# Memory-attention scores by seven products of halves: one more stage of a hybrid decoder step brought to the seven-product scheme

## The chip, the cores and the metric

The kernel runs on one core of a Trainium2 chip, in one launch. Its engines work side by side, each through its own queue of instructions: TensorE (PE in the profile; its weight loads are listed as PEld), VectorE (DVE), ScalarE (ACT), GpSimd (POOL) and SyncE (SP), which here issues the DMA transfers. The metric is device time in microseconds, lower is better.

## What is computed

One layer of a decoder for a prompt of 2048 tokens of width 1024, and for 8 x 4 new tokens of other requests. A mixer (gated linear attention beside a spatial-gating MLP) and its output projection are followed by a cross attention over 256 memory tokens, and by a gated feed-forward part with a short convolution. The change is about the cross attention of the prompt:

```python
def mem_attend(hn, mk, mv, wq_x, wo_x):
    B, T, _ = hn.shape
    q = (hn @ wq_x).reshape(B, T, MEM_HEADS, MEM_DH)
    s = jnp.einsum('bthd,bmhd->bhtm', q, mk).astype(jnp.float32) * (MEM_DH ** -0.5)
    p = jax.nn.softmax(s, axis=-1).astype(mv.dtype)
    o = jnp.einsum('bhtm,bmhd->bthd', p, mv).reshape(B, T, D_MODEL)
    return o @ wo_x
```

Here `hn` is the normed residual, there are 4 heads of 256, and `mk`, `mv` are projections of the 256 memory tokens. All values are float32.

## The kernel before

**Precision.** Each float32 matrix product is made of three matmuls on operands split into a high and a low part (`mm3`, lines 92 to 94: high by high, high by low, low by high). A split (`split`, lines 84 and 85) is a copy on ScalarE for the high part and a subtraction on VectorE for the low one.

**Tiling.** The prompt is worked in four sub-blocks of 512 tokens. In a sub-block: input projection, mixer, output projection (`w1`, `w2`: tiles `a_wo`), scores (`sc`), softmax, turning of the probabilities (`pT`), attention output (`x1`, `x2`: tiles `a_wx`), feed-forward (`a_wg`, `a_wup`, `d`). The 32 other tokens ride with the second and third sub-block.

**Folded keys.** In the first sub-block the query weights are multiplied with the keys once (`turn_wq`, `fold_qk`), head by head, so that the scores of two heads are the product of the tokens (512 x 1024) and a matrix of 1024 x 512, two heads of 256 memory tokens. The folded keys are split, written to DRAM (`qkd`) and read back in every sub-block, high and low part (`wready`). The values are folded with the output weights in the same way (`vod`).

**Scores.** Step `score(i, j)` takes two heads (i) and a quarter of the 1024 rows (j). For each of four chunks of 128 tokens it accumulates into one PSUM bank: tokens are the stationary operand, 512 key columns the moving one. At the last quarter `soften` takes maxima from PSUM, exponentiates into a scratch tile and divides by the sum. `turn` transposes the probabilities on TensorE.

**Tokens.** `out_proj_steps` adds the projection to the residual, column block m by column block, and calls `finish(m)`: scaling by the norm's gain, the split, the square, and the sum of the squares on GpSimd. The row scale of the norm is applied later, in the softmax.

**Seven products.** The feed-forward stage of sub-blocks 1 to 3 multiplies 2 x 2 blocks by seven products instead of eight (`seven_step`), with sums and differences of blocks on both sides. `seven_tokens` makes those of the tokens from an even and an odd column block (the halves of the contraction) and two halves of the tokens, as the split operands named A11, S1, A12, S2, S3, S4, A22. The sums of the weights were made once and lie in DRAM.

**Order and buffers.** `run` walks through a list of steps and issues the loads of the steps ahead (`AHEAD = 5` units); `weave` mixes side steps into the main list. The compiler's scheduler then orders each engine's instructions along a simulated timeline, so neighbours in the program may change places. Buffers that matter: 5 each of high weights, low weights and raw weights, 49 tiles of 128 x 544 (`U`), 6 scratch tiles of that size (`T_`), 4 key reload tiles (`X`), 4 PSUM banks for accumulators (`acc`) and 4 for the rest (`mps`).

Of the kernel before, what the change touches and what calls it, by code (L numbers as in the profile page):

```python
# [37 lines left out]
def hymba_step_kernel(  # L38
# [142 lines left out]
    def seven_tokens(a, b, H, name):  # L181

        B11, B12, B21, B22 = a[:, :H], a[:, H:2 * H], b[:, :H], b[:, H:2 * H]
        t13, t24 = T_(f"t13{name}"), T_(f"t24{name}")
        lo_, hi_ = slice(0, H), slice(H, 2 * H)
        dve.tensor_tensor(t13[:, lo_], B12, B11, ALU.subtract)
        dve.tensor_tensor(t13[:, hi_], B22, B12, ALU.subtract)
        dve.tensor_tensor(t24[:, lo_], B22, t13[:, lo_], ALU.subtract)
        dve.tensor_tensor(t24[:, hi_], B21, t24[:, lo_], ALU.subtract)
        one = U(f"w1{name}", F32R)  # L190
        split(one[:, lo_], one[:, hi_], B11)
        out = {"A11": (one[:, lo_], one[:, hi_])}
        for nm, src, first, second in (("b", b, "A12", "S4"), ("t", t13, "S1", "S3"), ("u", t24, "S2", "A22")):
            h, l = U(f"w{nm}h{name}", F32R), U(f"w{nm}l{name}", F32R)
            split(h[:, :2 * H], l[:, :2 * H], src[:, :2 * H])
            out[first], out[second] = (h[:, lo_], l[:, lo_]), (h[:, hi_], l[:, hi_])
        return out
# [296 lines left out]
    qkd = [[dp.tile([128, 2, 2, 512], F32, tag=f"qkd{i}{j}", name=f"qkd{i}{j}") for j in range(4)] for i in range(2)]  # L494
# [86 lines left out]
    def turn_wq(h, j, raw):  # L581

        out = []
        if j == 0:
            again("k", h)
# [9 lines left out]
    def fold_qk(h, j):  # L595

        kh, kl = mem_st.t["k"]
        w = mem_st.t.pop(("w", h, j))
        flush()
        for kk in range(2):  # L600
            ps = mps(f"qkp{h}{j}{kk}")
# [6 lines left out]
            hi, lo = U(f"qkh{h}{j}{kk}", F32R), U(f"qkl{h}{j}{kk}", F32R)  # L608
            split(hi[:, :512], lo[:, :512], ps)
            for x, t in enumerate((hi, lo)):  # L610
                put(qkd[h // 2][2 * j + kk][:, x, :, (h % 2) * 256:(h % 2 + 1) * 256],
                    t[:, :512].bitcast(F32).rearrange("p (k m) -> p k m", k=2))
# [27 lines left out]
    for h in range(4):  # L640
        for j in range(2):
            qk_steps.append(Step(lambda a, h=h, j=j: turn_wq(h, j, a), [wraw_unit(wq_x[0], 4 * j, 4, h * 256, 256, f"wqf{h}{j}")]))
            qk_steps.append(Step(lambda h=h, j=j: fold_qk(h, j)))
# [535 lines left out]
    def out_proj_steps(B, unit, src, g, name, sample, first, finished, keep=None, seven=False,  # L1179
# [35 lines left out]
        def finish(m):  # L1215
            if seven:
                t = T_(f"{name}g{s}{m}")
                act.activation(t[:, :T], B.h[m][:, :T], AF.Copy, scale=gcol(g, m))
                if m % 2:
                    B.hn.append(seven_tokens(B.even, t, T // 2, f"{s}{m}"))  # L1220
                else:
                    B.even = t
# [35 lines left out]
    def attention_steps(B):  # L1258
# [15 lines left out]
        def score(i, j):  # L1274

            def fn(wu):
                wh, wl = wu
                for c in range(4):
                    cs = slice(c * 128, (c + 1) * 128)
                    if j == 0:  # L1280
                        B.p[i, c] = acc(f"sc{s}{i}{c}")
                    ps = B.p[i, c]
                    for kk in range(2):
                        k = 2 * j + kk
                        mm3(ps, B.hn[k][0][:, cs], B.hn[k][1][:, cs], wh[:, kk], wl[:, kk], k == 0, k == 7)
                    if j == 3:
                        soften(i, c, ps)
            return Step(fn, [wready(qkd[i][j], f"qk{s}{i}{j}")])

        def soften(i, c, ps):  # L1290

            mx = narrow(f"mx{s}{i}{c}")
            dve.tensor_reduce(mx[:, 0:2], ps.rearrange("p (t m) -> p t m", t=2), AX.X, ALU.max)
            dve.tensor_scalar(mx[:, 0:2], mx[:, 0:2], B.rn[:, c:c + 1], None, ALU.mult)
            p = T_(f"p{s}{i}{c}")
            for hh in range(2):
                hs_ = slice(hh * 256, (hh + 1) * 256)
                act.activation(p[:, hs_], ps[:, hs_], AF.Exp,
                               bias=mx[:, hh:hh + 1], scale=B.rp[:, c:c + 1], accum_out=mx[:, 2 + hh:3 + hh])
            dve.reciprocal(mx[:, 4:6], mx[:, 2:4])  # L1300
            for hh in range(2):
                pt = p[:, hh * 256:(hh + 1) * 256]
                dve.tensor_scalar(pt, pt, mx[:, 4 + hh:5 + hh], None, ALU.mult)
            B.p[i, c] = p

        def turn(h):
            for mt in range(2):
                ps = mps(f"pT{s}{h}{mt}")
                for c in range(4):
                    a = (h % 2) * 256 + mt * 128  # L1310
                    pe.transpose(ps[:, c * 128:(c + 1) * 128], B.p[h // 2, c][:, a:a + 128], ident)
# [4 lines left out]
        return Step(scales), [score(i, j) for i in range(2) for j in range(4)], [Step(lambda h=h: turn(h)) for h in range(4)]  # L1316
# [341 lines left out]
    for s, B in enumerate(blocks):  # L1658
# [5 lines left out]
        if B.mix_sample:  # L1664
            def keep():
                if not hasattr(smp, "x"):
# [3 lines left out]
                                      lambda B=B: B.cat, "gx", "wo", B.mix_sample, 4, B.mix_sample, keep)  # L1670
# [6 lines left out]
        steps += weave(sc + x1, (turns[:2], 4, 5), (turns[2:], 8, 8))  # L1677
# [49 lines left out]
```

## Time and profile before

| | |
|---|---|
| median of 3 runs | 2845.88 us (2843.69 to 2846.43) |
| the profiled execution | 2846.04 us, of which the span is 2844.3 |
| mean granted clock of TensorE | 0.997 |
| score stages (first to last score matmul) | 324.8 to 371.9, 1028.4 to 1076.1, 1722.3 to 1769.3, 2393.7 to 2440.5 us |
| DMA | 625.54 MB, 219 GB/s over the span |

A row of a group names the line, engine, operation, what is written and read, the shape and the count; then the busy time in us and the mean duration of one in ns; then how long the engine had been idle before, and what ended that. Durations of matmuls overlap: what one costs is the distance to the next.

### The profile page before, as it was taken

What the parts mean: (1) busy time and instruction counts of PE and PEld (TensorE: products, weight loads), DVE (VectorE), ACT (ScalarE), POOL (GpSimd) and SP (SyncE); (2) the same over time, 40 slices, a digit from 0 to 9 for tenths busy, and PEclk for the clock granted to TensorE, in tenths of its full rate; (3) what the DMA queues carried; (4) which work ended last, traced back from release to release, by engine and by line L of the source; (5) the groups of instructions that cost most, each with busy time, mean ns of one, the idle gap of its engine ahead of it and who ended that gap; (6) DMA issues with size and microseconds to landing.
All of it is one profiled execution on the core that took longest, in us unless ns stands there. A gap on an engine that the chain in (4) does not pass through costs nothing.

```text
span 2844.3 us, 45766 instructions
## 1 busy us (share of the span) xinstructions
PE 2814.4 (99%) x17366; PEld 2457.6 (86%) x17366; DVE 1773.6 (62%) x3160; ACT 1047.0 (37%) x1942; POOL 542.4 (19%) x617
## 2 busy tenths in 40 slices
PE   8999999999999999999999999999999999999998
PEld 8788888888888898898888888899999888899998
DVE  6577468777657735555555773666666674565555
ACT  5536334333363424222124443422223543331221
POOL 1002113111110211322220021322221012131221
PEclk9999999999999999999999999999999999999999
DMA  9656679999932245888994215577776323577784
GB/s 304 207 156 199 208 228 332 335 340 329 345 112 77 94 153 178 302 284 291 329 344 161 73 60 181 191 259 257 257 263 213 104 69 119 185 258 269 273 286 173
DMA packets 363920, 625.54 MB, mean 220 GB/s; under 512 B 26730, under 2 KB 235724, under 8 KB 363702
## 3 DMA queue, kind: packets, MB, share of 16 engines
q1 hardware_dynamic: 363702, 622.62, 64.6%
q8 instruction: 138, 2.26, 0.3%
q14 instruction: 80, 0.66, 0.1%
HBM read 497.21 MB, written 125.31 MB: 219 GB/s over the span
## 4 chain that ended last, share of the span: by engine, by line
PE 95%; DVE 2%; DMA 1%; ACT 1%; issue 1%; POOL 0%; SPq 0%; DVEq 0%; POOLq 0%; ACTq 0%
PE d L92 6%; PE d L94 6%; PE d L93 6%; PE a_wo L92 2%; PE a_wo L94 2%; PE a_wo L93 2%; PE sc L94 2%; PE sc L93 2%; PE sc L92 2%; PE a_wx L93 2%; PE a_wx L94 2%; PE a_wx L92 2%; PE s L1022 2%; PE a_wg L92 1%; PE a_wup L92 1%; PE a_wg L93 1%
## 5 line engine op out<-in xcount | busy, mean ns | idle before, releaser
L92 PE MATMUL d<-acth,whi_wd 128*128 128x512 f32 (+2 forms) x720 | 244.6, 340 | 0.5 <-DVE h L1581 0.5
L93 PE MATMUL d<-actl,whi_wd 128*128 128x512 f32 (+2 forms) x720 | 242.5, 337 | 0.0
L94 PE MATMUL d<-acth,wlo_wd 128*128 128x512 f32 (+2 forms) x720 | 242.0, 337 | 0.0
L1581 DVE TENSOR_TENSOR h<-d,h 128x512 f32<-128x512 f32 (+1 forms) x232 | 133.4, 582 | 139.6 <-PE d L94 139.4
L1520 POOL TENSOR_TENSOR c<-c,bc_f 128x512 f32<-128x512 f32 (+1 forms) x88 | 138.5, 1578 | 137.9 <-ACT c L1519 137.2
L94 PEld LDWEIGHTS d<-acth,wlo_wd 128*128 128x128 f32 x720 | 135.4, 188 | 15.3 <-issue 1.2
L92 PEld LDWEIGHTS d<-acth,whi_wd 128*128 128x128 f32 x720 | 135.3, 188 | 14.4 <-DVE h L1581 0.7
L93 PEld LDWEIGHTS d<-actl,whi_wd 128*128 128x128 f32 x720 | 135.6, 188 | 13.8 <-issue 0.4
L1510 ACT ACTIVATE c<-g,colsb 128x512 f32<-128x512 f32 x88 | 71.7, 815 | 203.7 <-DVE g L1479 151.8
L1542 POOL TENSOR_TENSOR c<-r_q_wup,c 128x512 f32<-128x512 f32 (+1 forms) x33 | 59.1, 1790 | 333.5 <-DVE r_q_wup L279 213.1
L92 PE MATMUL a_wo<-ch,h_wo 128*128 128x512 f32 (+1 forms) x320 | 112.7, 356 | 4.5 <-DVE r L828 4.5
L1507 POOL COPY carry<-g 128x2 f32<-128x2 f32 x88 | 30.7, 349 | 436.5 <-DVE g L1479 434.4
L94 PE MATMUL a_wo<-ch,l_wo 128*128 128x512 f32 (+1 forms) x320 | 112.4, 353 | 0.0
L93 PE MATMUL a_wo<-cl,h_wo 128*128 128x512 f32 (+1 forms) x320 | 112.0, 351 | 0.0
L1511 DVE SCALAR_TENSOR_TENSOR c<-g,colsb,c 128x512 f32<-128x512 f32 x88 | 86.0, 977 | 29.3 <-ACT c L1510 28.8
L92 PE MATMUL sc<-whi_qk,woh 128*128 128x512 f32 x256 | 102.1, 399 | 0.0
L92 PE MATMUL a_wx<-pTh,whi_wx 128*128 128x512 f32 x256 | 101.3, 396 | 0.0
L94 PE MATMUL sc<-whi_qk,wol 128*128 128x512 f32 x256 | 101.1, 397 | 0.0
L93 PE MATMUL a_wx<-pTl,whi_wx 128*128 128x512 f32 x256 | 101.1, 395 | 0.0
L93 PE MATMUL sc<-wlo_qk,woh 128*128 128x512 f32 x256 | 101.0, 395 | 0.0
L94 PE MATMUL a_wx<-pTh,wlo_wx 128*128 128x512 f32 x256 | 100.6, 393 | 0.0
L84 ACT ACTIVATE acth<-c 128x512 fp32r<-128x512 f32 (+1 forms) x88 | 55.9, 636 | 110.4 <-DVE c L1542 85.0
(3369 smaller groups left out, 9204.8 us busy)
## 6 DMA issues: line engine op xcount, KB each, us to landing
whi_wd<-wd SPq DMA_DIRECT2D x66, 512.0 KB
wlo_wd<-wd SPq DMA_DIRECT2D x66, 512.0 KB
r_wo<-in_w_out_dram SPq DMA_DIRECT2D x32, 512.0 KB
whi_qk<-qkd SPq DMA_DIRECT2D x32, 512.0 KB
wlo_qk<-qkd SPq DMA_DIRECT2D x32, 512.0 KB
wlo_wx<-vod SPq DMA_DIRECT2D x32, 512.0 KB
whi_wx<-vod SPq DMA_DIRECT2D x32, 512.0 KB
r_wg<-in_w_gate_dram SPq DMA_DIRECT2D x22, 512.0 KB
```

The source lines that it names most:

```text
L84: act.activation(hi, src, AF.Copy)
L92: pe.matmul(ps, wh, xh, start=first, stop=False)
L93: pe.matmul(ps, wh, xl, start=False, stop=False)
L94: pe.matmul(ps, wl, xh, start=False, stop=last)
L1022: pe.matmul(ps3[:, :, c * 64:(c + 1) * 64], kl[:, c * 128:(c + 1) * 128], kr3[:, :, c * 64:(c + 1) * 64], start=True, stop=True)
L1507: pool.tensor_copy(carry[:, f, :], g[:, SB:SB + 2])
L1510: act.activation(c[:, :SB], g[:, 2:SB + 2], AF.Identity, bias=cb, scale=w2)
L1511: dve.scalar_tensor_tensor(c[:, :SB], g[:, 1:SB + 1], w1, c[:, :SB], ALU.mult, ALU.add)
L1520: pool.tensor_tensor(c[:, :T], c[:, :T], B.fbc[:, :T], ALU.mult)
L1542: (dve, pool)[i].tensor_tensor(c[:, :T], q[i], c[:, :T], ALU.mult)
L1581: dve.tensor_tensor(B.h[m + mm][:, cs], ps[:, :cw], B.h[m + mm][:, cs], ALU.add)
```

## The change

The scores of two heads become seven products of quarter blocks. On the key side the blocks are even and odd 128-row blocks of an even and an odd head; on the token side even and odd column blocks for the first and the second 256 tokens. `fold_qk` now writes three plain blocks, split (`plain`), and four sums, unsplit (`sums`), which are split each time they are read. Two heads are folded in turn, so the keys are reloaded at each fold. The output projection of every sub-block makes its tokens by `seven_tokens`, whose operations are in another order, for the last pair with a part split off (`apart`). The scores are put together from the products by VectorE in scratch tiles, and the softmax works in them in place. The turning steps come later in the list.

```diff
@@ seven_tokens
-    def seven_tokens(a, b, H, name):
+    def seven_tokens(a, b, H, name, apart=False):
...
+        one = U(f"w1{name}", F32R)
+        split(one[:, lo_], one[:, hi_], B11)
+        out = {"A11": (one[:, lo_], one[:, hi_])}
         dve.tensor_tensor(t13[:, lo_], B12, B11, ALU.subtract)
+        th, tl = U(f"wth{name}", F32R), U(f"wtl{name}", F32R)
+        if apart:
+            split(th[:, lo_], tl[:, lo_], t13[:, lo_])
         dve.tensor_tensor(t13[:, hi_], B22, B12, ALU.subtract)
         dve.tensor_tensor(t24[:, lo_], B22, t13[:, lo_], ALU.subtract)
         dve.tensor_tensor(t24[:, hi_], B21, t24[:, lo_], ALU.subtract)
...
-        for nm, src, first, second in (("b", b, "A12", "S4"), ("t", t13, "S1", "S3"), ("u", t24, "S2", "A22")):
-            h, l = U(f"w{nm}h{name}", F32R), U(f"w{nm}l{name}", F32R)
-            split(h[:, :2 * H], l[:, :2 * H], src[:, :2 * H])
+        for nm, src, first, second in (("b", b, "A12", "S4"), ("u", t24, "S2", "A22"), ("t", t13, "S1", "S3")):
+            if nm == "t":
+                h, l, c = th, tl, slice(H if apart else 0, 2 * H)
+            else:
+                h, l, c = U(f"w{nm}h{name}", F32R), U(f"w{nm}l{name}", F32R), slice(0, 2 * H)
+            split(h[:, c], l[:, c], src[:, c])
@@ turn_wq
-        if j == 0:
-            again("k", h)
+        again("k", h)
@@ fold_qk
-            hi, lo = U(f"qkh{h}{j}{kk}", F32R), U(f"qkl{h}{j}{kk}", F32R)
-            split(hi[:, :512], lo[:, :512], ps)
+            f, hi, lo = U(f"qkf{h}{j}{kk}"), U(f"qkh{h}{j}{kk}", F32R), U(f"qkl{h}{j}{kk}", F32R)
+            act.activation(f[:, :512], ps, AF.Copy)
+            m0, m1 = slice(0, 256), slice(256, 512)
+            if h % 2 == 0:
+                mem_st.t["f", jj] = f
+                split(hi[:, :512], lo[:, :512], f[:, :512])
+                for x, t in enumerate((hi, lo)):
+                    put(plain[:, 0:2, x, jj], t[:, :512].bitcast(F32).rearrange("p (s m) -> p s m", s=2))
+                continue
+            e = mem_st.t.pop(("f", jj))
+            split(hi[:, m1], lo[:, m1], f[:, m1])
             for x, t in enumerate((hi, lo)):
...
+                put(plain[:, 2, x, jj], t[:, m1].bitcast(F32))
+            t13, t24 = U(f"q13{h}{j}{kk}"), U(f"q24{h}{j}{kk}")
+            dve.tensor_tensor(t13[:, m0], f[:, m0], f[:, m1], ALU.add)
+            dve.tensor_tensor(t13[:, m1], e[:, m0], f[:, m0], ALU.subtract)
+            dve.tensor_tensor(t24[:, m0], t13[:, m0], e[:, m0], ALU.subtract)
+            dve.tensor_tensor(t24[:, m1], e[:, m1], t24[:, m0], ALU.subtract)
+            for i, t in enumerate((t13, t24)):
+                put(sums[:, 2 * i:2 * i + 2, jj], t[:, :512].rearrange("p (s m) -> p s m", s=2))
@@ attention_steps
-        def score(i, j):
+        SEQ = ("A11", "S1", "A12", "S2", "S3", "S4", "A22")
+        def score(i, nm):
+            plain, sums = q7d[i]
             def fn(wu):
                 wh, wl = wu
-                for c in range(4):
+                if nm == "A11":
+                    B.p[i], B.ps = [None] * 4, {}
+                ps = B.ps[nm] = acc(f"sc{s}{i}{nm}")
+                for c in range(2):
                     cs = slice(c * 128, (c + 1) * 128)
...
-                        mm3(ps, B.hn[k][0][:, cs], B.hn[k][1][:, cs], wh[:, kk], wl[:, kk], k == 0, k == 7)
+                    for k in range(4):
+                        xh, xl = B.hn[k][nm]
+                        mm3(ps[:, c * 256:(c + 1) * 256], xh[:, cs], xl[:, cs], wh[:, k], wl[:, k], k == 0, k == 3)
+                q = B.p[i]
+                plus = lambda o, nm, b: dve.tensor_tensor(q[o][:, :512], B.ps[nm], q[b][:, :512], ALU.add)
+                if nm == "A11":
+                    q[0] = T_(f"p{s}{i}0")
+                    act.activation(q[0][:, :512], ps, AF.Copy)
+                elif nm == "S2":
+                    q[3], q[1] = T_(f"p{s}{i}3"), T_(f"p{s}{i}1")
+                    plus(3, "S2", 0)
+                    plus(0, "A12", 0)
+                    plus(1, "S1", 3)
+                    soften(i, 0)
+                elif nm == "S3":
+                    q[2] = T_(f"p{s}{i}2")
+                    plus(2, "S3", 3)
+                    plus(3, "S3", 1)
+                    soften(i, 3)
+                elif nm == "S4":
+                    plus(1, "S4", 1)
+                    soften(i, 1)
+                elif nm == "A22":
+                    plus(2, "A22", 2)
+                    soften(i, 2)
+            def load():
+                if nm in PLAIN:
+                    return wready(plain[:, PLAIN.index(nm)], f"qk{s}{i}{nm}")()
+                raw = wraw(f"qk{s}{i}{nm}")
+                nc.sync.dma_start(raw[:, :1024], sums[:, SUMS.index(nm)].rearrange("p k m -> p (k m)"))
+                return wsplit(raw[:, :1024].rearrange("p (k m) -> p k m", k=4), f"qk{s}{i}{nm}")
+            return Step(fn, [load])
@@ the list of steps
-        steps += weave(sc + x1, (turns[:2], 4, 5), (turns[2:], 8, 8))
+        steps += weave(sc + x1, (turns[:2], 8, 9), (turns[2:3], 13, 13), (turns[3:], 14, 14))
```

`soften(i, j)` now works on one quarter block, q[j]: two chunks of 128 tokens by one head of 256, with a row scale for each chunk. The order of the eight fold steps becomes: both heads of a pair at one half of the rows, then at the other. The output projection gets `seven=True` in all sub-blocks.

62 lines of the change are left out of this document (25 added, 37 removed).

## The prediction

> **What bounds the kernel now.** I read the engine totals of the page first, then its forty slices, then the list of waits of TensorE.
>
> ```profile
> span 2844.3 us, 45766 instructions
> PE 2814.4 (99%) x17366; PEld 2457.6 (86%) x17366; DVE 1773.6 (62%) x3160; ACT 1047.0 (37%) x1942; POOL 542.4 (19%) x617
> PEclk9999999999999999999999999999999999999999
> ```
>
> ```profile
> PE a_wo L92 <- DVE r L828: 4.5, 3, 2.0
> PE a_wg20S L93 <- DVE wtl L85: 1.0, 1, 1.0
> PE wxss L1242 <- POOL wxsq L1235: 0.9, 2, 0.5
> ```
>
> TensorE (PE) is busy 99% of the span at the full granted clock, and its longest wait in total is 4.5 us. So the time is the sum of what TensorE issues, and only fewer or cheaper matmuls, or new waits, can move it. The two last rows are the waits at the entry of the feed-forward stage, which already works by seven products: the nearest model of what the change builds for the scores.
>
> A busy share says nothing of the price of one matmul, because matmuls overlap. That comes from their distance, start to start:
>
> ```profile
> 2404.62 0.40 PE L93 MATMUL sc<-wlo_qk,woh 128*128 128x512 f32 x1
> ...
> 2406.46 0.39 PE L92 MATMUL sc<-whi_qk,woh 128*128 128x512 f32 x1
> ```
>
> ```profile
> 2509.74 0.28 PE L93 MATMUL a_wg31A<-w,wg31A 128*128 128x256 f32 x1
> ...
> 2510.70 0.28 PE L92 MATMUL a_wg31A<-w,wg31A 128*128 128x256 f32 x1
> ```
>
> Each pair of rows is eight steps apart: 1.84/8 = 0.230 us for a matmul of 512 columns, 0.96/8 = 0.120 us for one of 256. Whole stretches say nearly the same (start and length in us, then busy time and count of PE, PEld, DVE, ACT, POOL, the clock, the DMA share and GB/s):
>
> ```profile
> 2372.00:2393.60 21.60, 21.60 (x95) 17.51 (x94) 10.47 (x15) 8.72 (x14) 7.50 (x7) 1.00 0.57 195
> 2393.60:2440.70 47.10, 47.10 (x218) 38.59 (x217) 14.17 (x40) 11.81 (x31) 3.28 (x3) 1.00 0.53 179
> 2473.20:2484.20 11.00, 11.00 (x50) 8.92 (x49) 7.00 (x10) 4.58 (x8) 2.85 (x2) 1.00 0.59 195
> 2507.00:2517.00 10.00, 10.00 (x87) 10.00 (x86) 9.44 (x12) 4.64 (x7) 4.22 (x3) 1.00 0.76 261
> 2530.00:2540.00 10.00, 10.00 (x84) 9.91 (x83) 4.72 (x9) 1.53 (x3) 1.81 (x1) 1.00 1.02 404
> ```
>
> ```profile
> 2358.79 1.75 PE otp L1155 x16
> ```
>
> The first is the second half of the output projection in the last sub-block, the second its score stage: its 192 score matmuls and some 24 small ones, transposes mostly, at 0.11 us each by the last row (1.75/16, from the chain in order of time), so (47.10 - 2.7)/192 = 0.231. The fourth is pure 256-column work: 85 starts (two of the 87 began before it), 0.118 each.
>
> **The change, part by part. The products.** A sub-block's scores are now 2 x 4 x 4 x 2 x 3 = 192 matmuls of 512 columns; by seven products they are 2 x 7 x 2 x 4 x 3 = 336 of 256. I take 0.231 and 0.119, between the readings: 44.3 us becomes 40.0 us. That saves 4.3 us in each of four sub-blocks, **17.3 us** in all (by the ends of the readings 15.4 to 19.6). All of it lies on the path. The number of transposes, fold matmuls and projection matmuls stays.
>
> Does a weight load for every 256 columns cost more? There are 144 more loads per sub-block:
>
> ```profile
> L92 PEld LDWEIGHTS sc<-whi_qk,woh 128*128 128x128 f32 x256 | 48.4, 189 | 10.5
> ```
>
> A load lasts 189 ns, more than the 119 ns of a step, yet the fourth stretch holds 86 loads beside 87 matmuls in 10.00 us, so loads overlap matmuls and each other. The Trainium skill speaks against the change here (Perfetto Trace Analysis, Matmuls: larger matmuls are more efficient when possible; TensorE: Matmul & The Clock Gate, LDWEIGHTS: columns divided by 1.2 in ns, 107 ns for 128). By that figure, an estimate, 144 loads laid in series would add 15 us per sub-block; the trace disagrees for this shape.
>
> **Vector's bill.** Everything else the change adds lies on VectorE (DVE), ScalarE (ACT) and the queue of SyncE, beside TensorE. So I count whether it fits. The rows:
>
> ```profile
> L1208 DVE TENSOR_TENSOR h<-a_wo,h 128x512 f32<-128x512 f32 x48 | 32.6, 687 | 28.9 <-PE a_wo L94 28.8
> L85 DVE TENSOR_TENSOR l_wo<-r_wo,h_wo 128x1024 fp32r<-128x1024 f32 x32 | 39.2, 1225 | 3.6 <-ACT h_wo L84 3.6
> L84 ACT ACTIVATE h_wo<-r_wo 128x1024 fp32r<-128x1024 f32 x32 | 33.8, 1056 | 65.8 <-PE a_wo L93 36.0 <-PE t_wr L94 23.7 <-issue 3.5
> L189 DVE TENSOR_TENSOR t<-wxg,t x12: 416/1003/1602, 1098.3 to 2491.4; 128x256 f32<-128x256 f32 x8, 128x272 f32<-128x272 f32 x4
> L1235 POOL TENSOR_TENSOR wosq<-wosq,woq 128x512 f32<-128x512 f32 x21 | 27.2, 1296 | 33.0 <-ACT woq L1230 33.0
> ```
>
> (a) Tokens. seven_tokens already runs after the attention's output projection; the third stretch holds one pair of it, residual adds included, for 7.0 us of VectorE. Four pairs in the output projection's second half cost 28.0 us where 10.5 stand now. PE passes a pair in 24 x 0.231 = 5.5 us, so VectorE falls behind there. (b) Eight loaded sums per sub-block are split on the way in, each 1.06 us of ScalarE and 1.23 us of VectorE: 9.8 us. (c) Fourteen 512-column sums out of PSUM, by the residual add's 0.687 us: 9.6 us. (d) The softmax keeps its operations, in place: 14.2 us less the 1.4 of the last residual add and token split, 12.8 us. Sum 60.2 us, against 21.6 + 40.0 = 61.6 us of TensorE. ScalarE gets 4 x 4.58 = 18.3 for the pairs (third stretch), 11.8 as now in the score stage, 8.5 for the eight splits and 1.2 for two copies out of PSUM: 39.8 of 61.6.
>
> So VectorE just fits, nearly full for a whole stretch. That alone need not stop TensorE: in the fourth stretch VectorE is busy 9.44 of 10.00 us and TensorE all of it. It costs where PE must have an operand or a bank soon:
>
> - **Entry.** VectorE meets the last pair after 2.8 us of idling, 28.0 of pairs and 2.4 of two splits: some 33 us after the projection's second half began, 11.5 us after PE left it. PE can run A11 and S1, which need the even tile alone, and the first three k of A12 and S2: 2 x 2.86 + 2 x 2.14 = 10.0 us. Then it waits up to 1.5 us. The feed-forward's like entry waits 0.5 and 1.0 us (the rows above). I take 1.0.
> - **Banks.** S4 needs an accumulator of the first four products back. After S2, three sums of 0.69 us, 2.06 together, come before S1's bank is free, and S3 lasts 2.86 us. A split of 1.23 us in front makes it 0.4 us late. Behind those sums on VectorE stand the softmax and the next splits. Twice per sub-block: 0.7 with the ACT hops; nothing if no split is in front.
>
> Cost 1.7 us per sub-block, 6.8 us in all; ends nothing and the whole 4.3 (17.3).
>
> **The softmax's end.** Its last two sums and softmaxes come after the last product. The turned tiles of heads 2 and 3 are first used when two steps of the attention's output projection are past, 2 x 24 x 0.231 = 11 us later. About 6 us of VectorE work stand before them: nothing. Without this cover it would cost those 6 us per sub-block.
>
> **DMA.** Keys come as 10.5 MB instead of 8.4 per sub-block (six products of two 512 KB tiles, eight of one), in 40.0 instead of 44.3 us: 262 GB/s against the 179 of the second stretch. The fifth stretch moves 404 GB/s with TensorE full, so the rate is there. With five buffers each way, a load is asked for four products (11 us) ahead; the shortest wait chain in it is a load, 1.06 and 1.23 us. Nothing, if a load takes under 9 us.
>
> **The first sub-block's folds.** Each of eight folds now reloads its keys (4 more pairs of 256 KB loads), sixteen tiles are copied first, and the odd heads make four sums:
>
> ```profile
> 75.00:200.00 125.00, 122.74 (x712) 104.99 (x712) 78.78 (x141) 63.32 (x128) 7.18 (x4) 0.99 0.59 187
> L84 ACT ACTIVATE qkh<-qkp 128x512 fp32r<-128x512 f32 x16 | 9.2, 593 | 3.5 <-PE qkp L94 3.0 <-ACT e L1039 0.4
> 2.46 5.04 DMA mx<-in_mem_prompt_dram
> ```
>
> In the stretch of the folds ScalarE gets 16 x 0.59 less 1.5, some 8 us more on 63, VectorE 8 x (4 x 0.42 - 0.27) = 11 us on 79, of 125. The input projection covers both. Reloads queue on SyncE behind the writes of earlier folds, and the projection's weights queue behind them; a 256 KB load took 5.04 us, so four uncovered ones cost 20 us at the worst. The fold of one step waits for them while the projection's matmuls run: I take 1 us. More scratch tiles live at once there; of this I take nothing apart.
>
> **Sum**, against the profiled execution's 2846.04 us (span 2844.3; the median of the runs is 2845.88, so both readings agree): 2846.0 - 17.3 + 6.8 + 1.0 = **2836.5 us**. About 0.2% (5.7 us) is what a measurement of this kernel can tell from no change, so 2840.3 and 2851.7 are the bounds between faster, same and slower.
>
> **The rivals.** *All of it arrives.* PE's order fills the entry with other products and no bank is late: 2846.0 - 17.3 = 2828.7. For it: VectorE at 9.44 of 10 beside a full PE. Against: VectorE idles first and is behind by 11 us at the entry. *Given back.* Each sub-block loses at entry and banks 3.3 to 4.3 us, what it saves, and the folds cost 1 to 3: 2846.0 - 17.3 + 13 to 17 + 1 to 3 = 2843 to 2849, say 2845. It needs a VectorE bill some 2 us longer than mine. The row of L189 shows a way: an operation of 0.42 us at its shortest has a median of 1.00 where GpSimd's squares are summed beside it, 1.3 us each. My 7.0 us per pair hold two such collisions at 0.6 to 1.1; eight in the output projection at the full 1.3 would be 10.4 instead of some 7, and the bill 3 us longer. The Trainium skill has this as a rule (SBUF — State Buffer, Who interferes with whom): a VectorE operation with both inputs in SBUF and a GpSimd operation that reads SBUF exclude each other from a shared port for a whole instruction. By that rule, which the trace bears out at L189, it would be this rival and 2845. *VectorE becomes the bound* (the slower side). If the slow form of L189 hit the four small sums and the A11 split of every pair, 5 x 4 x 0.59 = 11.8 us per sub-block, the bill is 72.0 against 61.6: PE waits 10.4, less 4.3, six us lost per sub-block, 24 in all, 2870 us. It decides against the change from a bill of 67 us up (61.6 + 4.3, and 1.4 for the measurable bound). Against it: ten operations of the third stretch already include two collisions and sum to 7.0. *The change isn't what it says*: the steps of 256 are bound by loads in series, 336 x 0.189 = 63.5 us instead of 44.3, 77 us more, 2923; the fourth stretch excludes it nearly.
>
> **How the numbers follow.** Forecast (2831 to 2840.3) 0.40; all of it (below 2831) 0.22; given back (2840.3 to 2851.7) 0.23; VectorE the bound 0.13, uncovered reloads 0.01, loads 0.01. So faster 0.62, same 0.23, slower 0.15. The range leaves out the slow cases and the utmost end of the readings (2846.0 - 19.6): 2827 to 2851. The likeliest sign is faster, its own range 2827 to 2840.
>
> **What would show it.** Right: sc matmuls x1344 of 128x256 with 0.119 us between starts; score stages of 40 to 42 us; VectorE busy over 85% from the projection's second half to the scores' end; waits of PE's sc rows for VectorE, together under 7 us, at S2's or S4's first matmuls. Wrong: score stages over 44 us; PE waiting on a DMA of keys or on an h/l tile of a sum; a hole of PE between 75 and 200 us beyond the 2.3 of now; the output projection's second half longer than 21.6 us because residual adds come late.

## The result, and the profile after

| | before | after |
|---|---|---|
| median of 4 runs each, side by side | 2844.78 us (2843.63 to 2846.43) | 2861.59 us (2859.08 to 2863.04) |
| ratio to before, 95% interval | | 1.0059 [1.0045, 1.0072] |
| the profiled execution, and its span | 2846.04, 2844.3 us | 2863.04, 2861.1 us |
| mean granted clock | 0.997 | 0.993 |

The change makes the kernel slower by 0.6%, about 17 us, where 9.5 us of gain were forecast. The totals of the page of after, to be laid beside those of before:

```profile
span 2861.1 us, 47430 instructions
PE 2811.7 (98%) x17942; PEld 2483.2 (87%) x17942; DVE 1906.5 (67%) x3380; ACT 1126.6 (39%) x2068; POOL 544.4 (19%) x617
```

TensorE is busy 2.7 us less, not 17 us less, and the span is 16.8 us longer. So two things are wrong at once: the expected saving isn't visible in TensorE's own busy time, and TensorE stands still longer. The stages tell where. First the four score stages of after, each from the first to the last score matmul (start and end, length; busy time and count of PE, PEld, DVE, ACT, POOL; clock; DMA share and GB/s):

```profile
331.30:381.40 50.10, 45.87 (x361) 44.42 (x360) 38.88 (x77) 25.10 (x53) 5.46 (x4) 0.97 0.67 228
1036.50:1085.90 49.40, 45.22 (x366) 43.61 (x364) 39.34 (x83) 24.64 (x52) 6.02 (x5) 1.00 0.65 218
1733.30:1783.80 50.50, 47.01 (x361) 45.38 (x360) 38.70 (x77) 24.96 (x53) 5.47 (x4) 0.93 0.57 197
2405.80:2456.00 50.20, 46.80 (x361) 45.17 (x360) 38.22 (x77) 24.83 (x53) 5.77 (x4) 0.93 0.56 197
sum 200.20, PE 184.88 PEld 178.58 DVE 155.15 ACT 99.52 POOL 22.72; mean PE 46.22 PEld 44.64 DVE 38.79 ACT 24.88 POOL 5.68
```

Before, the same four stages sum to 188.6 us (from the four stages of the table of before). Together they are 11.6 us longer, although each should have become 4.3 us shorter. In every one TensorE stands still for 3.4 to 4.2 us (the length less PE's busy time), and in three of them the clock is below 1.00. The rest of the 16.8 us lies ahead of the first sub-block's output projection. Its first and last start, before and after:

```profile
L92 PE MATMUL a_wo<-ch,h_wo x64: 390/393/496, 276.0 to 324.1; 128*128 128x512 f32 x64
```

```profile
L92 PE MATMUL a_wo<-ch,h_wo x64: 390/392/504, 282.3 to 330.6; 128*128 128x512 f32 x64
```

The projection begins 6.3 us later. 11.6 and 6.3 are 17.9; everything else gives 1 us back.

**Inside a score stage.** The list of waits of TensorE in after names what it stands still for (line and tile, what it waits for; us in total, times, longest). Its longest rows for score matmuls, and one of the short ones:

```profile
PE sc10A L94 <- DVE w1wo L85: 1.8, 2, 0.9
PE sc00A L92 <- DVE h L1232: 1.4, 1, 1.4
PE sc20A L92 <- DVE h L1232: 1.2, 1, 1.2
PE sc30A L92 <- DVE h L1232: 1.2, 1, 1.2
PE sc20S L92 <- ACT wthwo L84: 0.6, 1, 0.6
```

All of the score rows are waits at the entry, 15 us together. Those for `w1wo`, `wthwo` and the like are for tokens. Those for `h L1232`, 5.0 us in the four stages, are for accumulators, as the timeline below shows. None is for keys from DRAM or for an h or l tile of a key sum. The windows of the stage of sub-block 2 agree: 5 us with half the clock, and later 10 us in which nothing is lost.

```profile
1743.00:1748.00 5.00, 4.59 (x22) 4.30 (x21) 3.02 (x6) 1.58 (x2) 0.53 (x1) 0.50 0.09 36
1763.00:1773.00 10.00, 10.00 (x87) 10.00 (x86) 6.28 (x16) 5.94 (x15) 0.00 (x0) 1.00 0.39 116
```

In the second of these 87 matmuls start or run in 10.00 us, which is the pace the forecast took from the feed-forward stage. The products are cheap; the entry is not. The timeline of TensorE at that entry (start, duration, engine, line, what is written and read, and in brackets the wait before it):

```profile
1733.31 0.29 PE L92 MATMUL sc20A<-whi_qk20A,w1wo 128*128 128x256 f32 x1
...
1734.97 0.28 PE L94 MATMUL sc20S<-h_qk20S,wtlwo 128*128 128x256 f32 x1
1736.45 0.39 PE L92 MATMUL sc20A<-whi_qk20A,wbhwo 128*128 128x256 f32 x1 [1.20 <-DVE h L1232]
...
1737.98 0.39 PE L92 MATMUL sc20S<-h_qk20S,wuhwo 128*128 128x256 f32 x1 [0.21 <-DVE h L1232]
...
1743.87 0.58 PE L94 MATMUL sc20A<-whi_qk20A,w1wo 128*128 128x256 f32 x1 [0.41 <-DVE w1wo L85]
1744.25 0.42 PE L92 MATMUL sc20A<-whi_qk20A,w1wo 128*128 128x256 f32 x1
1744.46 0.41 PE L93 MATMUL sc20A<-wlo_qk20A,w1wo 128*128 128x256 f32 x1
```

From 1733.31 on TensorE issues 15 matmuls: nine of A11 and six of S1, all of them for the first 128 tokens. Then, after 1.66 us of starts, it waits for the first time. The second 128 tokens of A11, whose first three k are ready by 1734.03, begin only at 1744.25, right after the last step of the first 128 tokens. Both chunks lie in one PSUM bank, each with a start of its own. The last two rows are 0.21 us apart, where the pace is 0.12: the clock is halved. The queue of VectorE shows what came so late:

```profile
1734.29 1.50 DVE L195 TENSOR_TENSOR t24wo<-wog,t13wo 128x256 f32<-128x256 f32 x1
1735.72 0.68 DVE L1232 TENSOR_TENSOR h<-a_wo,h 128x512 f32<-128x512 f32 x1
...
1737.25 0.68 DVE L1232 TENSOR_TENSOR h<-a_wo,h 128x512 f32<-128x512 f32 x1
1737.85 1.53 DVE L190 TENSOR_TENSOR t13wo<-wog 128x256 f32<-128x256 f32 x1
...
1742.32 1.50 DVE L85 TENSOR_TENSOR w1wo<-wog,w1wo 128x256 fp32r<-128x256 f32 x1
...
1745.35 0.68 DVE L85 TENSOR_TENSOR wulwo<-t24wo,wuhwo 128x512 fp32r<-128x512 f32 x1
```

Two residual adds of the last column blocks stand in front of the fourth pair, and small operations of 0.41 us become 1.50 where GpSimd adds a square. VectorE is through at 1746.0, 12.7 us after TensorE left the projection at 1733.3.

The same two adds explain the first wait. The four accumulators are used in turn, so A11, S1, A12 and S2 follow on column blocks 4 to 7 of the projection. A12 (`wbhwo`) can't begin before the add of block 6 has read its sum, nor S2 (`wuhwo`) before that of block 7 has. They start at 1736.45 and 1737.98, just after these adds end (1735.72 and 1737.25, and 0.68 each), although the operands of their first k were ready long before. Sub-blocks 0 and 3 show the same two waits; in sub-block 1 it is S1 that waits, 0.6 us. The profile doesn't name the banks; that they go in turn is read from the program and agrees with these times.

### The profile page after: what moved, and what is told of

Its sections match the earlier page's. It is cut to its first block, busy times and chain, and to the rows that moved or that the text cites. A ratio compares the mean times of both kernels' runs of the same rounds, so it can differ in the third digit from the quotient of the medians.

```text
span 2861.1 us, 47430 instructions
## 1 busy us (share of the span) xinstructions
PE 2811.7 (98%) x17942; PEld 2483.2 (87%) x17942; DVE 1906.5 (67%) x3380; ACT 1126.6 (39%) x2068; POOL 544.4 (19%) x617
## 4 chain that ended last, share of the span: by engine, by line
PE 91%; DVE 5%; DMA 1%; ACT 1%; issue 1%; POOL 0%; SPq 0%; DVEq 0%; POOLq 0%; ACTq 0%
PE d L94 6%; PE d L92 6%; PE d L93 6%; PE a_wx L92 2%; PE a_wx L94 2%; PE a_wx L93 2%; PE s L1046 2%; PE a_wup L94 1%; PE a_wg L94 1%; PE a_wg L92 1%; PE a_wup L92 1%; PE a_wup L93 1%; PE a_wg L93 1%; PE a_wo L92 1%; PE a_wo L93 1%
## 5 line engine op out<-in xcount | busy, mean ns | idle before, releaser
L93 PEld LDWEIGHTS d<-actl,whi_wd 128*128 128x128 f32 x720 | 135.5, 188 | 14.1 <-issue 0.4
L1566 DVE SCALAR_TENSOR_TENSOR c<-g,colsb,c 128x512 f32<-128x512 f32 x88 | 86.0, 977 | 29.3 <-ACT c L1565 28.7
L1574 ACT ACTIVATE c<-c 128x512 f32<-128x512 f32 (+1 forms) x88 | 56.2, 638 | 105.9 <-DVE c L1567 94.2
L1567 DVE SCALAR_TENSOR_TENSOR c<-g,colsb,c 128x512 f32<-128x512 f32 x88 | 93.8, 1066 | 1.1
L85 DVE TENSOR_TENSOR actl<-c,acth 128x512 fp32r<-128x512 f32 (+1 forms) x88 | 64.7, 738 | 24.2 <-ACT acth L84 23.2
```

The source lines that it names most:

```text
L85: (lo_eng or dve).tensor_tensor(lo, src, hi.bitcast(F32), ALU.subtract)
L93: pe.matmul(ps, wh, xl, start=False, stop=False)
L1566: dve.scalar_tensor_tensor(c[:, :SB], g[:, 1:SB + 1], w1, c[:, :SB], ALU.mult, ALU.add)
L1567: dve.scalar_tensor_tensor(c[:, :SB], g[:, 0:SB], w0, c[:, :SB], ALU.mult, ALU.add)
L1574: act.activation(c[:, :T], c[:, :T], AF.Gelu_apprx_tanh)
```

## The experiments

Two theories for the score stages. **Cover:** VectorE's tail is of the forecast length, but TensorE has far less to do meanwhile than was counted, because what it may issue is set by the chunks, banks and the order of the queue. **Port:** GpSimd's sums of squares stretch VectorE's operations, so the tokens come too late whatever TensorE has. They aren't exclusive, so each experiment removes one and leaves the other. A third question is the 6 us at the folds.

All medians below stand beside runs of the kernel before on the same chip (2843.65 to 2843.79 us, by group). Beside after the kernel before took 2844.78, so a difference from after is about 1 us too large. "Stages" is the sum of the four score stages, 200.2 us in after and 188.6 in before.

**1. Tokens spaced out.** `w1[i]` and `w2[i]` are the first and second half of the contraction for column blocks 2i and 2i + 1. Two steps of the first half are held back, so that the last two pairs come ready half as densely.

```diff
-        steps += weave(proj + w1, *folds, ...
+        steps += weave(proj + w1[:2], *folds, ...
...
-        steps += w2 + [stat, scales]
+        steps += w2[:2] + [w1[2], w2[2], w1[3], w2[3], stat, scales]
```

> The change, with two steps of the output projection moved: the first halves of the last two column pairs come between their second halves, so that the last two token pairs follow each other at 11 us instead of 5.5. Nothing is left out. Theory 1 (entry: VectorE still works off the token pairs when the scores begin, TensorE idles some 3.5 us and then runs some 7 us at half clock, 7 to 8 us lost per sub-block): the score stages shrink from about 50.3 us to 43 to 45, and the time falls by 22 to 30 us to some 2832 to 2840. Theory 2 (the products themselves cost more than the feed-forward's, by banks or VectorE's sums): the score stages stay at 49 us or more and the time within 5 us of 2861.

Measured: 2843.25 us, ratio 0.9998 [0.9988, 1.0007], 18.3 us less than after.

```profile
sum 176.00, PE 173.14 PEld 171.22 DVE 135.81 ACT 92.97 POOL 15.87; mean PE 43.29 PEld 42.80 DVE 33.95 ACT 23.24 POOL 3.97
```

The stages lose 24.2 us, and TensorE's idle time in them falls from 15.3 to 2.9 us. No matmul and no operation is added or removed: only the order of the list is another. The spans of the two profiled executions differ by 23.5 us (2861.1 and 2837.6): 24.2 in the stages and 3.2 ahead of the first output projection, which begins at 279.1 us in place of 282.3, less 3.9 elsewhere. The medians differ by 18.3 only, because after's profiled execution was the longest of its four and this one the shortest of its ten.

**2. Without GpSimd's sums.** Seven of the eight sums of each output projection are left out, so the norm's scale, and with it what the kernel computes, is another. The run only prices the sums.

```diff
-            else:
+            elif name == "wx":
                 pool.tensor_tensor(B.sq[:, :T], B.sq[:, :T], t[:, :T], ALU.add)
```

> The change without seven of the eight sums of squares that GpSimd makes in each output projection (the norm's scale then comes from one column block alone). If the operations of VectorE that meet those sums are what makes it late (eight of 0.6 to 1.1 us per sub-block), VectorE's token work ends some 5 to 7 us earlier, the half-clock stretch goes and the score stages shrink to 44 to 47 us, 14 to 24 us in all. If VectorE is late by its own operations and the order in its queue, the score stages shrink by 1 us or less.

Measured: 2832.57 us, ratio 0.9958 [0.9941, 0.9974], 29.0 us less than after. The effect is larger than expected. The stages sum to 167.6 us, with no idle time of TensorE; one of them:

```profile
1719.30:1761.20 41.90, 41.90 (x354) 41.90 (x354) 31.89 (x70) 22.62 (x49) 1.15 (x1) 1.00 0.62 216
```

It holds 354 matmuls where after has 361: the other seven, small ones of the norm's sum, stand ahead of the stage here. The price of the sums shows in the groups of VectorE's operations with the same names, after first:

```profile
L195 DVE TENSOR_TENSOR t24wo<-wog,t13wo 128x256 f32<-128x256 f32 x16 | 14.3, 893 | 0.0
```

```profile
L195 DVE TENSOR_TENSOR t24wo<-wog,t13wo 128x256 f32<-128x256 f32 x16 | 6.7, 417 | 0.0
```

The same sixteen operations take 893 ns each with GpSimd's sums and 417 without. Over all token operations VectorE is busy 92.5 us in after and 67.5 here. Those 25.0 us by 28 sums (7 per sub-block) are 0.89 us of VectorE for each sum on GpSimd. In experiment 1 the token operations still take 88.3 us: there the stretching stays, and only the lateness at the entry goes.

**3. The same sums on VectorE**, which gives it more to do and takes GpSimd away from beside it.

```diff
-                pool.tensor_tensor(B.sq[:, :T], B.sq[:, :T], t[:, :T], ALU.add)
+                (dve if name == "wo" else pool).tensor_tensor(B.sq[:, :T], B.sq[:, :T], t[:, :T], ALU.add)
```

> The change with the sums of squares of the output projection made on VectorE instead of GpSimd: the same work, but VectorE gets eight operations of 0.6 us more per sub-block (4.8 us) and GpSimd never reads SBUF beside it. Theory A (the two engines hold each other up: a GpSimd sum costs VectorE more than doing the sum itself): the score stages shrink from 50 to 43 to 46 us and the time falls by 12 to 28 us, to 2833 to 2850. Theory B (without those sums VectorE simply had less to wait for in its order, no mutual hold-up): the added 4.8 us make the stages longer than 50 us and the time 2861 or more.

Measured: 2840.73 us, ratio 0.9985 [0.9975, 0.9995], 20.9 us less than after; stages 179.8 us. The sums take, on VectorE,

```profile
L1259 DVE TENSOR_TENSOR wosq<-wosq,woq 128x512 f32<-128x512 f32 x21 | 14.3, 683 | 0.0
```

and 5.0 us for the seven of 544 columns. With 67.3 us of token operations that is 86.6 us, 5.9 less than the 92.5 of after, with 28 operations more. GpSimd's help costs VectorE more than doing the work itself. But 1.5 us per sub-block doesn't by itself explain 5 us per stage. The entry of sub-block 2 shows more of it:

```profile
1724.97 0.28 PE L92 MATMUL sc20A<-whi_qk20A,w1wo 128*128 128x256 f32 x1
...
1726.62 0.28 PE L92 MATMUL sc20A<-whi_qk20A,wbhwo 128*128 128x256 f32 x1
...
1727.81 0.28 PE L92 MATMUL sc20S<-h_qk20S,wuhwo 128*128 128x256 f32 x1
...
1730.71 0.39 PE L94 MATMUL sc20S<-h_qk20S,wulwo 128*128 128x256 f32 x1 [0.67 <-DVE wulwo L85]
```

Here the two residual adds end at 1724.50 and 1727.31, ahead of A12 and of S2, so neither waits for its accumulator, and 36 matmuls run before the first listed wait. VectorE is through 11.8 us after TensorE left the projection, not 12.7. That the adds come earlier because the order is easier to plan without the stretches is argued, not shown.

**4. The sums of squares after the projection.** The squares are made in `stat`, held there by a scale that is read from the last column block.

```diff
         def stat():
+            if name == "wo":
+                one = narrow(f"one{s}")
+                dve.tensor_scalar(one[:, 0:1], B.h[7][:, 0:1], 0.0, 1.0, ALU.mult, ALU.add)
+                for m in range(8):
+                    square(m, one[:, 0:1])
```

> The change with the squares and their sums moved behind the last residual add of the output projection (their scale is a one made from that add's result), so that GpSimd sums beside the scores instead of beside the token pairs. Nothing is left out. Theory A: VectorE keeps up with the pairs, the score stages are 43 to 46 us, the time 2833 to 2850, limited by the softmax, which then waits for the norm's scale until some 14 us into the stage. Theory B (the tail of VectorE's work is there anyway): 48 us or more per stage, within 8 us of 2861.

Measured: 2838.73 us, ratio 0.9983 [0.9973, 0.9992], 22.9 us less than after; stages 179.0 us. Here the work is kept and GpSimd keeps its part, only later. No wait for tokens at the entry is longer than 0.2 us. A new wait takes up part of the gain, once in each stage: S3 takes the accumulator of A11, and ScalarE's copy of that product out of PSUM comes late.

```profile
PE sc20S L92 <- ACT p L1328: 1.6, 1, 1.6
```

**5. Chunks of tokens inside, k outside.** The run that tells cover from port: the bank is opened once and closed once, so that TensorE can work at both chunks with what is ready. VectorE's and GpSimd's instructions stay.

```diff
-                for c in range(2):
-                    cs = slice(c * 128, (c + 1) * 128)
-                    for k in range(4):
-                        xh, xl = B.hn[k][nm]
-                        mm3(ps[:, c * 256:(c + 1) * 256], xh[:, cs], xl[:, cs], wh[:, k], wl[:, k], k == 0, k == 3)
+                for k in range(4):
+                    xh, xl = B.hn[k][nm]
+                    for c in range(2):
+                        cs = slice(c * 128, (c + 1) * 128)
+                        mm3(ps[:, c * 256:(c + 1) * 256], xh[:, cs], xl[:, cs], wh[:, k], wl[:, k], k + c == 0, k + c == 4)
```

> The change with the loops of a product exchanged: rows of the contraction outside, the two chunks of tokens inside, both in one open accumulation group of the bank. Nothing is left out. In the change a bank's second chunk cannot begin before the first chunk has its last pair of columns, so at the entry only some 31 matmuls (3.7 us) of the first four products can run ahead of the last token pair; now it is 72 (8.6 us). Theory C (the loss is that missing cover, whatever makes VectorE late): the stages shrink from 50 to 43 to 46 us, the time to 2833 to 2848. Theory A alone (VectorE's tail of 12 to 13 us sets the stage, cover or not): 48 us or more and 2853 or more.

Measured: 2844.56 us, ratio 1.0002 [0.9992, 1.0012], 17.0 us less than after. One stage, and the entry of it, TensorE's timeline and then VectorE's two residual adds and last token operation:

```profile
1724.60:1769.70 45.10, 43.38 (x361) 42.76 (x360) 38.12 (x77) 24.78 (x53) 6.83 (x4) 1.00 0.63 219
```

```profile
1724.58 0.29 PE L92 MATMUL sc20A<-whi_qk20A,w1wo 128*128 128x256 f32 x1
...
1728.17 0.28 PE L92 MATMUL sc20A<-whi_qk20A,wbhwo 128*128 128x256 f32 x1
...
1730.57 0.28 PE L94 MATMUL sc20S<-h_qk20S,wulwo 128*128 128x256 f32 x1
1731.60 0.39 PE L92 MATMUL sc20S<-h_qk20S,wthwo 128*128 128x256 f32 x1 [0.74 <-ACT wthwo L84]
```

```profile
1726.99 0.68 DVE L1232 TENSOR_TENSOR h<-a_wo,h 128x512 f32<-128x512 f32 x1
...
1728.52 0.68 DVE L1232 TENSOR_TENSOR h<-a_wo,h 128x512 f32<-128x512 f32 x1
...
1736.60 0.68 DVE L85 TENSOR_TENSOR wulwo<-t24wo,wuhwo 128x512 fp32r<-128x512 f32 x1
```

TensorE now issues 51 matmuls over 6.0 us ahead of its first wait, where it had 15 over 1.7. VectorE ends its tokens 12.7 us after TensorE left the projection (1737.3 less 1724.6), just as late as in after, and is as busy in the stage (38.1 against 38.7 us). The two adds end 3.1 and 4.6 us after TensorE left the projection, as in after, but A12 now comes 3.6 us after it and S2 5.8, so neither waits for its accumulator. So the same lateness costs far less once TensorE has cover: idle time in the four stages falls from 15.3 to 7.1 us, and TensorE's busy time from 184.9 to 174.7, as the clock stays at 1.00 in all four. The exchange changes the order of the chunks and the moment at which the accumulators are asked for at once; what each is worth alone isn't shown.

**6. The former order of the token operations** (b, t, u; nothing split off).

```diff
-        for nm, src, first, second in (("b", b, "A12", "S4"), ("u", t24, "S2", "A22"), ("t", t13, "S1", "S3")):
+        for nm, src, first, second in (("b", b, "A12", "S4"), ("t", t13, "S1", "S3"), ("u", t24, "S2", "A22")):
...
-                    B.hn.append(seven_tokens(B.even, t, TH // 2, f"{name}{s}{m}", name == "wo" and m == 7))
+                    B.hn.append(seven_tokens(B.even, t, TH // 2, f"{name}{s}{m}", False))
```

> The change with the token sums split in the feed-forward's former order (S1 and S3 before S2 and A22) and without the part split off for the last pair; A11 stays first. If that order at the entry matters, it is worse by 1 us or more per score stage (2865 or more); if VectorE's total is what counts, it stays within 4 us of 2861.

Measured: 2856.09 us, ratio 1.0045 [1.003, 1.006], 5.5 us less than after, against what was expected. The order that came with the change, t last, is likely the worse one: the profiled stages sum to 191.7 us in place of 200.2, but the intervals of the two ratios overlap (after's is [1.0045, 1.0072]). Part of the gain is the clock. One stage stands still as long as its like in after (3.4 against 3.5 us) at full clock:

```profile
1728.90:1776.70 47.80, 44.43 (x361) 43.00 (x360) 37.90 (x76) 24.83 (x51) 5.19 (x4) 1.00 0.60 208
```

**7. Sums split once, when they are folded.** The loads of sums are then ready pairs like the others, and VectorE has 9.8 us less per stage by the forecast's bill.

```diff
-            dp.tile([128, 4, 4, 256], F32, tag=f"q7s{i}", name=f"q7s{i}")) for i in range(2)]
+            dp.tile([128, 4, 2, 4, 256], F32, tag=f"q7s{i}", name=f"q7s{i}")) for i in range(2)]
...
+                split(sh[:, :512], sl[:, :512], t[:, :512])
...
-                return wsplit(raw[:, :1024].rearrange("p (k m) -> p k m", k=4), f"qk{s}{i}{nm}")
+                return wready(sums[:, SUMS.index(nm)], f"qk{s}{i}{nm}")()
```

> The change with the four sums of the folded keys stored split, as high and low part, so that none is split when it is read (four more 512 KB transfers for each pair of heads, sixteen more splits in the folds). If the splits of the loaded sums on VectorE (three of them, 1.2 us each, lie between the token operations at the entry) carry the loss, the score stages shrink by 3 us or more each, 12 us in all, less what the folds then cost more (0 to 3 us). If they are only a part: 1 to 2 us each. If DMA is short, the stages grow.

Measured: 2848.59 us, ratio 1.0016 [1.0007, 1.0026], 13.0 us less than after. The stages fall to 178.6 us, but the first projection starts 10 us later still, at 292.6 us. The folds lengthen far more than the 0 to 3 us expected. One part of the 10 us is TensorE's longest wait there, after first:

```profile
PE qkp L92 <- ACT wqh L84: 1.8, 1, 1.8
```

```profile
PE qkp L92 <- ACT wqh L84: 5.4, 1, 5.4
```

**8. Keys reloaded once per head**, with the fold order of before.

```diff
-        again("k", h)
+        if j == 0:
+            again("k", h)
...
-    for h, j in ((2 * i + hh, j) for i in range(2) for j in range(2) for hh in range(2)):
+    for h, j in ((h, j) for h in range(4) for j in range(2)):
```

> The change with the folds in the order of before, head by head, and the keys loaded once per head. If the reloads in a stretch where the DMA engines are full (100 to 120 us) hold up the input projection's weights, which made TensorE wait and lose half its clock, the start of the first output projection comes 3 to 5 us earlier (282.3 to about 278) and the time falls by 3 to 5 us. If the added copies and sums do it, it stays within 1.5 us. The score stages stay at 50 us in either case.

Measured: 2860.91 us, ratio 1.006 [1.0045, 1.0075]: by the medians 0.7 us less than after, which decides nothing. Its profile says more: the first output projection starts at 277.6 instead of 282.3 us. One window of the folds, after first and then this kernel:

```profile
110.00:120.00 10.00, 6.94 (x35) 4.40 (x34) 2.43 (x5) 7.08 (x13) 0.00 (x0) 0.50 1.00 325
```

```profile
110.00:120.00 10.00, 8.49 (x40) 4.79 (x41) 3.67 (x8) 8.56 (x28) 0.00 (x0) 0.83 0.75 253
```

In after the DMA engines are full (share 1.00), TensorE stands still for 3.1 of 10 us and runs at half clock; with half the reloads it is 0.75, 1.5 us and 0.83. Just ahead of the window ScalarE stands still for a tile of the input projection's weights, and the split that the fold waits for comes behind it:

```profile
107.73 1.06 ACT L84 ACTIVATE h_wv<-r_wv 128x1024 fp32r<-128x1024 f32 x1 [3.42 <-DMA r_wv<-in_w_in_dram]
108.69 0.58 ACT L84 ACTIVATE wqh<-wqp 128x512 fp32r<-128x512 f32 x1
```

To settle it, the same edit was put on experiment 1.

> The change with the spaced token pairs and the keys loaded once per head. If both effects add up: 2843.3 less 1 to 5 us, 2838 to 2842. If the folds don't matter (the medians of the single change differed by 0.7 us only), 2842 to 2845.

Measured: 2838.37 us, ratio 0.9981 [0.9972, 0.9991], against 2843.25 without it: 4.9 us. The reloads, with the order of the folds that needs them, cost about that much.

**9. All three together**: 1, 8 and the sums of squares on VectorE as in 3.

> As the run before, with the sums of squares on VectorE. With pairs 11 us apart VectorE has room for them. Theory A: the last 2 us of waiting per score stage go (43.5 to 44.4 us become 42), 5 to 9 us less than the run before, some 2831 to 2836: faster than the kernel before. Theory B: no gain, or up to 5 us more.

Measured: 2832.32 us (2831.05 to 2835.92), ratio 0.9965 [0.9952, 0.9979]: faster than both kernels. That is 11.3 us less than before by the medians, and 15.0 by the spans of the profiled executions (2844.3 and 2829.3). The entry is clean, at full clock:

```profile
1715.60:1758.10 42.50, 42.50 (x361) 42.50 (x360) 32.18 (x69) 21.68 (x45) 1.01 (x1) 1.00 0.65 224
sum 170.80, PE 170.80 PEld 170.59 DVE 128.48 ACT 86.67 POOL 4.56; mean PE 42.70 PEld 42.65 DVE 32.12 ACT 21.67 POOL 1.14
```

**10. The late sums in place of VectorE's** (1, 8 and 4).

> The change with spaced token pairs, keys loaded once per head, and the squares made behind the last residual add. If GpSimd's reads beside the token pairs are the remaining cost, it does as well as the run with the sums on VectorE (2832 within 3 us) or better, since VectorE is spared 4.8 us per sub-block; if the late norm scale holds the softmax up, the score stages are 44 us and more, the time 2836 to 2842.

Measured: 2840.23 us, ratio 0.9988 [0.9979, 0.9998]. It is 8 us worse than 9: TensorE stands still for 1.9 to 2.1 us in each stage, mostly the same wait of 1.6 us for A11's accumulator as in 4.

**11. Kernel 9 with k outside** as in 5.

> Spaced pairs, keys once, sums of squares on VectorE, and the exchanged loops. The stages of that combination without the exchange have no idle time left (42.4 to 43.1 us), so all theories expect no change: 2832 within 3 us.

Measured: 2832.03 us, ratio 0.9961 [0.9946, 0.9976], the same as 9. Where the tokens come in time, the cover has nothing left to hide.

## Why the prediction was wrong, step by step

- **The products: right.** The kernel of experiment 9 runs the changed stage undisturbed, in 170.8 us for four against 188.6 of before: 17.8 us where 17.3 were forecast. (As a whole it gains less, 11.3 us by the medians; where the rest goes isn't shown.) The loads overlap, as forecast: 360 of them in 42.50 us of a TensorE that never stands still.
- **Vector's bill: right in size.** VectorE is busy 17.4 us in the projection's second half and 38.7 in the stage, 56.1 in place of 60.2; and it is through 12.7 us after TensorE left, where 11.5 were forecast. *VectorE becomes the bound* falls with it: its bill had to be 67.
- **Entry: the step that failed, by its size.** 1.0 us was put down, and the stages stand 29.4 us above those of experiment 9, 7.4 us each. The forecast said that TensorE could run A11 and S1 and the first three k of A12 and S2, "10.0 us. Then it waits up to 1.5 us". It counted what depends on the early tokens and not what TensorE can issue. Of those 10.0 us it issued 1.7 ahead of the first wait. The second chunk of a bank came only after the first; A11's own last part, which needs the even tile alone, stood nearly last in VectorE's queue, at 1742.3; and A12 and S2 needed accumulators that two residual adds in the same queue had to empty. Even with k outside, 6.0 us were issued and not 10.0: the third k of S1 wasn't split yet (the wait for `wthwo` at 1731.60). The 1.0 us leaned on the feed-forward's entry, but there a pair of token tiles comes every 11.0 us (the forecast's third stretch), and here every 5.5. Experiment 5 shows what the cover is worth: with VectorE as late and as busy, three and a half times the cover takes back 17.0 us. Experiment 1, with the same chunks but spaced tokens, takes back 18.3. The 29.4 us are 15.3 of waits (3.8 per stage) and 14.1 of longer busy time. Of these, a clock that halves after the waits in three of the four stages makes some 8.5 (1 less the clock, by the length: 1.5 to 3.5 us in those stages), and the forecast had no such term. The rest, some 5.6, is the halting itself, as far as the rows tell: around the wait listed as 1.20 us the starts are 1.48 us apart and the next two 0.22, where the pace is 0.12.
- **The rival *given back*: right mechanism, too small a price.** GpSimd's sums stretch VectorE's token operations, 25.0 us in all, 6.2 per sub-block, more than the 3 us of that rival. The Trainium skill's rule (SBUF — State Buffer, Who interferes with whom), by which VectorE work with two inputs in SBUF contends with GpSimd's reads for a shared pair of ports, agrees with experiments 2 and 3: 893 ns become 417, and VectorE is less busy with 28 more operations. It made VectorE late; the lack of cover made that cost time. Either cure alone takes back 17 us or more.
- **Banks: looked for in the wrong place.** 0.7 us per sub-block was put down for S4, and no S4 waits for its accumulator in after. The waits for accumulators stand at the entry, some 1.2 us per sub-block, where the forecast asked for operands only. With a clean entry nothing stands still at all.
- **The softmax's end and DMA: right**, at nothing: TensorE never waits for keys in the score stages, which move 197 to 228 GB/s.
- **The first sub-block's folds: 1.0 us forecast, about 5 measured.** Experiment 8 takes 4.7 of the 6.3 us off the start of the first projection, and its repeat 4.9 us off the median. The forecast looked at the whole stretch of 125 us, in which DMA has room, and not at the ten in which it has none. Of the remaining 1.6 us the cause stays open. The list's order plays into it too: experiment 1 leaves the folds as they are, and the projection begins 3.2 us earlier.

What the four sizes give: 17.8 saved, 29.4 lost at the entry, 6.3 ahead of the first projection and 1.1 back elsewhere make the 16.8 us of the spans.

## What to carry to other kernels

At the entry of a stage, don't count the matmuls whose operands are ready. List them in the order in which the engine may issue them (chunk, accumulator that must be emptied first, queue of the producer), and compare that time with the producer's tail. If the tail is longer, spread the producer's work over the stage before, or put the loop over k outside, rather than make the producer a little faster. A sum handed to GpSimd beside two-input VectorE work can cost VectorE more than the sum itself, here 0.89 us against 0.68.

## What the runs showed of the hardware

**The clock.** In the entry of sub-block 2 TensorE waited several times within 9 us, at most 1.20 us at a time and some 3.5 us in all, and then ran at 0.50 for some 7 us (1741.4 to 1748.1), with starts 0.21 us apart instead of 0.12. Sub-block 1 stood still longer (4.2 us of its stage) and kept 1.00; so did the third stage in experiment 6, with 3.4 us. The Trainium skill names gaps of more than about 3 us as the danger (TensorE: Matmul & The Clock Gate, Why this matters for your kernels), and elsewhere on that page tells of frequent short idling between groups of matmuls that makes the clock go back and forth (A second HAM failure mode: psum-queue depth-cycling). What was seen here, with no gap above 1.20 us, is nearer the second. Which sequence of short waits halves the clock and which doesn't, these runs do not settle.

**A helper that costs more than it does.** The group of GpSimd's sums in after:

```profile
L1259 POOL TENSOR_TENSOR wosq<-wosq,woq 128x512 f32<-128x512 f32 x21 | 31.3, 1491 | 49.1 <-ACT woq L1254 49.1
```

A sum of 128 x 512 took 1.30 us before and 1.49 here, and each one added 0.89 us to VectorE's work beside it; VectorE needs 0.68 us for the same sum. The residual adds, which take one input from PSUM, weren't stretched: all 48 of 512 columns took at most 0.69 us, also the one at 1730.41, beside a GpSimd sum that ran from 1730.37 to 1731.67.
